# A two-layer diffusion trunk on one core: the program's blocks put in order by a timeline simulator instead of the core simulator

## The chip, the core and the metric

The kernel runs on one core of a Trainium2 chip. The metric is the device time of one execution in microseconds (us), as the median of several runs. The profile of before comes from one more execution, recorded by the hardware profiler; all starts and durations below are from it.

The engines carry their usual short names: PE is TensorE (matmuls and transposes; PEld its weight loads), DVE is VectorE, ACT is ScalarE, POOL is GpSimd, SP is SyncE, which here only issues DMAs. Each engine works through its own queue of instructions in the order in which the built program holds them; an instruction whose inputs are not ready holds up all that stand behind it in that queue.

## What is computed

One inference step of a trunk with two layers over 640 tokens: 512 sample tokens and 128 prompt tokens, model width 2048. Each layer is

```
mod   = silu(cond) @ ada_w + ada_b            # shift, scale, gate; one set for the sample, one for the prompt
h     = rms_norm(x) * (1 + scale) + shift
p     = h @ w_in                              # the columns are cut into q, k, v, gates and conv inputs
y     = concat(branches(p)) * silu(gates)
x     = x + gate * (y @ w_out)
```

The even layer (layer 0) has windowed grouped-query attention with a sink logit per head, and a gated depthwise convolution of width 3. The odd layer (layer 1) has differential attention (two softmax maps per head, an RMS norm of each head's output) and grouped-query attention with normed and rotated q and k over cached and new keys. The prompt attends to itself only. New keys and values of the prompt are outputs too.

## The kernel before

**Products.** Every float32 product is made of three float32r matmuls. `split` (L213, L214) cuts a tile into a high part, an ACT copy (L213), and a low part, a DVE subtraction (L214: `lo = x - hi`). The product is then wh times h-high, wh times h-low and wl times h-high. So each weight tile `raw` of 128x512, loaded by an SP DMA, costs one ACT copy into `wh` and one DVE subtraction into `wl` before PE can use it. The three matmuls are L248 to L250 (`proj_q`), L261 to L263 (`proj_parts`) and L526 to L528 (`run_pairs`, the output projection, which multiplies sums and differences of blocks of weights and of activations so that it needs fewer products). They accumulate in PSUM tiles `pa`, `pb`, `Sp` and `pq`, nearly always 128 by 320 (half of the tokens) to a matmul.

**Start.** The conditioning rows `rows_a` and `rows_b` are transposed on PE (L120, L121) into one PSUM tile `T`, from which DVE reads `sT`, the silu of the condition (L122), and `vec` (L123, L124). The PSUM tiles named `T` have two buffers, which every transposition of the kernel shares. `x_block` (L869 to L884) transposes x, four 128x128 blocks to a `T` (L875); L876 copies each `T` into `xT`, three of four on DVE and the fourth on ACT; L880 squares x on ACT for the norm. Then `ada_on_pe` multiplies the first ada weights (L163 loads `ada`, 1 MB a time; L166 multiplies; L169, L172 and L174 bring the result into columns). `h0_maker` (L913 to L922) makes the 16 tiles `h`; behind the last of them in the source, L922 negates the sink logits (`nsink<-sink`), which DMA brings.

**Lead stage and fill.** The input projections of layer 0 begin while the other ada blocks come in, in eight units. The remaining modulation is spread over layer 0 by `ada_on_dve` (L186 loads `adaw`, 512 KB a time into three buffers; L189 and L191 multiply and add on DVE, 240 of them L191).

**Attention.** `pair_gen` gives the steps of two heads: scores (L738 to L742), softmax (L705 and L709 on DVE, L712 on ACT, L716 and L718 on DVE, L797 on ACT), transposes of p (L726), the split of p into `pth` (ACT) and `ptl` (DVE), the weighing of v (L786 to L788). `diff_gen` (L1453 to L1475) combines the two maps of differential attention, norms the result `on` (L1460 to L1464) and transposes it back (L1470). Keys are made by a projection, transposes (L555), norm and rotation (L580 to L600) and transposes again (L608, L555), then split into `k0h`, `k0l`, `k1h`, `k1l`. In the source these steps are interleaved by hand with the projections of the next heads.

**Between the layers.** `make_form` (L1073 to L1075) makes the sums and differences for the output projection and splits them into tiles `T0` to `T7`; L1112 adds the gated result to x (`xr`); `h1_maker` (L1300, ACT L1302, L1304) makes the 16 tiles `h` of layer 1, each for several ranges of columns, from `w8`, `T1`, `T2`, `acc`, `T0` and `xr` tiles.

**What sets the order.** The source is written as generators that are stepped in turn, which fixes each instruction's place in the program. The context (`tile.TileContext`, L1647) takes each block of that program and orders it anew, engine by engine, by running it through a simulator with a model of what each instruction costs: what is ready first in the simulator, and earlier in the program, goes first. It also hands out buffers and semaphores. On the chip the order is then fixed.

## Time and profile before

| | us |
|---|---|
| median of 3 runs (2296.95 to 2298.61) | 2298.29 |
| the profiled execution | 2296.36 |
| its span, first to last instruction | 2294.5 |
| PE busy | 2255.1 |
| PE weight loads busy | 2178.4 |
| DVE busy | 1590.6 |
| ACT busy | 1089.8 |
| POOL busy | 160.5 |

The profiled execution lies 1.9 us under the median and 1.9 us over its own span. A busy time is the union of an engine's instructions in the span; matmuls overlap, so a busy PE need not be one at its best rate. The stages follow each other so: start and lead stage to about 187 us, even attention and convolution to about 930, output projection of layer 0 and the norm to about 1180, odd projections and attention to about 2085, the last output projection to the end.

### The profile page before, as it was taken

The page shows a single profiled execution, that of the slowest core. Times are in us where ns is not written, and L with a number is a line of the kernel's source. Part 1 is how long each engine was busy: PE and PEld are TensorE (multiplying, and loading weights), DVE is VectorE, ACT ScalarE, POOL GpSimd, SP SyncE. Part 2 cuts the span into 40 slices and gives each one's busy share as a digit, 9 for nine tenths or more (in the row PEclk, how much of TensorE's full clock was granted, in tenths as well). Part 3 has the DMA queues.
Part 4 walks back from the last instruction along what each step waited for, and adds up shares of the span by engine and source line. Part 5 has one row for each costly group of instructions (what it writes and reads, how often), then busy time and mean ns, then how long its engine had stood idle before and what let it go on. Part 6 is the DMA issues. An engine that isn't in the chain of part 4 may idle for free.

```text
span 2294.5 us, 41094 instructions
## 1 busy us (share of the span) xinstructions
PE 2255.1 (98%) x15900; PEld 2178.4 (95%) x15900; DVE 1590.6 (69%) x2831; ACT 1089.8 (47%) x2304; POOL 160.5 (7%) x224
## 2 busy tenths in 40 slices
PE   7999999999999999999999999999999999999999
PEld 5889899999999999999999999999999999999999
DVE  4666968779779777787796665365665655557875
ACT  5325652443522222444564443465565676755443
POOL 1001000000000000000100001011111100000101
PEclk9999999999999999999999999999999999999999
DMA  9985537547366564855553335223223211238642
GB/s 322 294 268 161 157 113 215 152 135 215 113 212 215 179 190 142 268 170 147 169 159 103 115 115 151 80 62 104 78 64 102 71 54 51 73 103 270 188 138 62
DMA packets 380900, 342.89 MB, mean 149 GB/s; under 512 B 16403, under 2 KB 338417, under 8 KB 380193
## 3 DMA queue, kind: packets, MB, share of 16 engines
q1 hardware_dynamic: 366288, 296.00, 42.9%
q0 software_dynamic: 13696, 42.10, 5.4%
q8 instruction: 125, 2.05, 0.4%
q10 hardware_dynamic: 720, 2.16, 0.3%
q14 instruction: 71, 0.57, 0.1%
HBM read 301.27 MB, written 38.93 MB: 148 GB/s over the span
## 4 chain that ended last, share of the span: by engine, by line
PE 84%; DVE 5%; ACT 4%; issue 3%; DMA 3%; POOL 1%; SPq 0%; POOLq 0%; ACTq 0%; DVEq 0%
PE pq L528 7%; PE pq L527 7%; PE pq L526 7%; PE pa L248 6%; PE pb L248 6%; PE pa L249 6%; PE pb L249 6%; PE pa L250 6%; PE pb L250 6%; PE pb L262 2%; PE pb L261 2%; PE pa L261 2%; PE pb L263 2%; PE pa L263 2%; PE pa L262 2%
## 5 line engine op out<-in xcount | busy, mean ns | idle before, releaser
L213 ACT ACTIVATE wh<-raw 128x512 fp32r<-128x512 f32 (+1 forms) x456 | 273.3, 600 | 578.4 <-PE pb L249 409.5
L214 DVE TENSOR_TENSOR wl<-raw,wh 128x512 fp32r<-128x512 f32 (+1 forms) x456 | 296.7, 652 | 214.7 <-ACT wh L213 194.2
L248 PE MATMUL pa<-h,wh 128*128 128x320 f32 x1024 | 326.0, 319 | 3.7 <-ACT h L213 2.3
L249 PE MATMUL pa<-h,wh 128*128 128x320 f32 x1024 | 319.2, 313 | 1.1 <-DVE h L214 1.0
L250 PE MATMUL pa<-h,wl 128*128 128x320 f32 x1024 | 318.7, 311 | 0.4 <-DVE wl L214 0.4
L249 PE MATMUL pb<-h,wh 128*128 128x320 f32 x1024 | 317.8, 310 | 0.0
L248 PE MATMUL pb<-h,wh 128*128 128x320 f32 x1024 | 317.6, 310 | 0.0
L250 PE MATMUL pb<-h,wl 128*128 128x320 f32 x1024 | 317.5, 310 | 0.0
L191 DVE SCALAR_TENSOR_TENSOR acc<-adaw,sT,acc 128x1024 f32<-128x1024 f32 x240 | 300.3, 1280 | 0.7 <-DMA adaw<-in_ada_w 0.7
L248 PEld LDWEIGHTS pa<-h,wh 128*128 128x128 f32 x1024 | 193.1, 189 | 17.8 <-issue 10.4
L526 PE MATMUL pq<-h,wh 128*128 128x320 f32 x640 | 199.0, 311 | 0.3 <-ACT wh L213 0.3
L249 PEld LDWEIGHTS pa<-h,wh 128*128 128x128 f32 x1024 | 193.3, 189 | 6.2 <-issue 3.3
L528 PE MATMUL pq<-h,wl 128*128 128x320 f32 x640 | 198.3, 310 | 0.1
L527 PE MATMUL pq<-h,wh 128*128 128x320 f32 x640 | 198.0, 309 | 0.0
L250 PEld LDWEIGHTS pa<-h,wl 128*128 128x128 f32 x1024 | 193.2, 189 | 2.7 <-issue 2.1
L249 PEld LDWEIGHTS pb<-h,wh 128*128 128x128 f32 x1024 | 192.6, 188 | 0.8 <-issue 0.8
L248 PEld LDWEIGHTS pb<-h,wh 128*128 128x128 f32 x1024 | 192.5, 188 | 0.7 <-issue 0.4
L250 PEld LDWEIGHTS pb<-h,wl 128*128 128x128 f32 x1024 | 192.6, 188 | 0.0
L527 PE MATMUL pq<-T,wh 128*128 128x320 f32 x480 | 148.1, 308 | 0.0
L528 PE MATMUL pq<-T,wl 128*128 128x320 f32 x480 | 147.9, 308 | 0.2 <-DVE wl L214 0.2
L526 PE MATMUL pq<-T,wh 128*128 128x320 f32 x480 | 147.8, 308 | 0.1
L261 PE MATMUL pa<-h,wh 128*128 128x320 f32 x432 | 141.2, 327 | 0.0
(431 smaller groups left out, 5311.3 us busy)
## 6 DMA issues: line engine op xcount, KB each, us to landing
adaw<-in_ada_w SPq DMA_DIRECT2D x128, 512.0 KB, 4.4
raw<-in_ev_w_in SPq DMA_DIRECT2D x176, 256.0 KB, 3.4
raw<-in_od_w_in SPq DMA_DIRECT2D x160, 256.0 KB, 2.9
ada<-in_ada_w SPq DMA_DIRECT2D x32, 1024.0 KB, 7.8
w<-in_od_w_in SPq DMA_DIRECT2D x24, 512.0 KB, 4.0
yd<-y POOLq DMA_DIRECT2D x32, 320.0 KB, 3.1
yin<-yd SPq DMA_DIRECT2D x32, 320.0 KB, 4.2
w<-yd SPq DMA_DIRECT2D x32, 320.0 KB, 4.0
```

The costliest lines, as they stand in the source:

```text
L191: V.scalar_tensor_tensor(out=acc[c], in0=w, scalar=sT[:, kt, c:c + 1], in1=acc[c], op0=ALU.mult, op1=ALU.add)
L213: A.activation(hi, x, AF.Copy)
L214: V.tensor_sub(lo, x, hi)
L248: PE.matmul(ps, wh[:, i, :], hi[:, sl], start=(j == js[0] if alone else (pos == 0 and j == 0)), stop=False)
L249: PE.matmul(ps, wh[:, i, :], lo[:, sl], start=False, stop=False)
L250: PE.matmul(ps, wl[:, i, :], hi[:, sl], start=False, stop=(j == js[1] - 1 if alone else (pos == 3 and j == 3)))
L261: PE.matmul(ps, wh[:, j, :], hi[:, sl], start=(qd == 0 and j == 0), stop=False)
L262: PE.matmul(ps, wh[:, j, :], lo[:, sl], start=False, stop=False)
L263: PE.matmul(ps, wl[:, j, :], hi[:, sl], start=False, stop=(qd == 3 and j == 3))
L526: PE.matmul(ps, wh[:, j, :], hi, start=(new and h == 0 and j == 0), stop=False, **kw)
L527: PE.matmul(ps, wh[:, j, :], lo, start=False, stop=False, **kw)
L528: PE.matmul(ps, wl[:, j, :], hi, start=False, stop=(h == 1 and j == 3), **kw)
```

## The change

One argument of the context is added. Nothing in the program's source, its tiles, pools or instructions differs.

```
-    with tile.TileContext(nc) as tc:
+    with tile.TileContext(nc, schedule_with_timeline_sim=True) as tc:
         trunk_kernel(tc, I, O)
```

The context now orders the blocks by a simulator of a timeline, with another model of costs. Both programs have the same instructions: 15533 on PE (matmuls), 2831 on DVE, 2098 on ACT, 851 DMA issues on SP, 227 on POOL. Of these, 8999 on PE stand at another place of their queue (by up to 351 places), 2157 on DVE (up to 206), 1424 on ACT (up to 60) and 571 on SP (up to 77). The moves fill the start and lead stage (the first 1000 or so PE instructions), even attention, the forms and the norm between the layers (on DVE), and odd attention; elsewhere the queues agree. Three places follow. A name's number tells one buffer's generation from another.

**DVE at the start.** Before, the three reads of `T_130` (the transposed conditioning rows) open the queue, ahead of the copies of x:

```order
L122 TENSOR_SCALAR sT_81<-T_130 128x16x2
L123 COPY vec_83<-T_130 128x80
L124 COPY vec_83<-T_130 128x77
L876 COPY xT0_206<-T_212 128x4x128
L882 TENSOR_REDUCE ssx_240<-s4_211 128x1
L883 TENSOR_SCALAR ssx_240<-ssx_240 128x1
L876 COPY xT1_207<-T_220 128x4x128
```

Now they stand behind a weight split, and behind DVE's first ten copies of x; the negation of the sink logits, whose data SP loads, comes a few rows later, ahead of the last five copies of x:

```order
L876 COPY xT0_206<-T_311 128x4x128
L214 TENSOR_TENSOR wl_459<-raw_450,wh_458 128x256
L122 TENSOR_SCALAR sT_81<-T_130 128x16x2
L123 COPY vec_83<-T_130 128x80
L124 COPY vec_83<-T_130 128x77
L214 TENSOR_TENSOR wl_463<-raw_452,wh_462 128x256
L214 TENSOR_TENSOR wl_467<-raw_454,wh_466 128x256
L922 TENSOR_SCALAR nsink_150<-sink_149 128x8
L876 COPY xT1_207<-T_319 128x4x128
L214 TENSOR_TENSOR wl_471<-raw_456,wh_470 128x256
L876 COPY xT2_208<-T_325 128x4x128
L876 COPY xT0_206<-T_344 128x4x128
```

So `sT` and the last parts of `xT`, which L166 needs, now come after `wl_459`, whose `raw_450` is a weight load, and after `sink`. `nsink` stood far behind, in the lead stage, before.

**DVE in the first pair of even attention.** Here `ptl_3102` and `ptl_3111` are splits of transposed p, which PE waits for; L191 is the modulation fill; `wl` rows split weights of later projections. Before, the rows around `ptl_3152`, the next split, are

```order
L214 TENSOR_TENSOR ptl_3152<-T_3148,pth_3151 128x256
L214 TENSOR_TENSOR wl_3392<-raw_3064,wh_3391 128x512
L971 TENSOR_TENSOR y_2595<-T_3135,y_2595 128x2x128
L716 TENSOR_TENSOR l_3127<-l_3127,es_3129 128x1
L191 SCALAR_TENSOR_TENSOR acc1_3036<-adaw_3644,sT_81,acc1_3036 128x1024
L718 RECIPROCAL rl_3132<-l_3127 128x1
L705 TENSOR_REDUCE nm_3167<-S_3159 128x1
L191 SCALAR_TENSOR_TENSOR acc0_3035<-adaw_3718,sT_81,acc0_3035 128x1024
L709 TENSOR_SCALAR nm_3167<-nm_3167,rq0_2687,nsink_150 128x1
L191 SCALAR_TENSOR_TENSOR acc1_3036<-adaw_3718,sT_81,acc1_3036 128x1024
L214 TENSOR_TENSOR ptl_3185<-T_3179,pth_3184 128x512
```

and now the rows ahead of `ptl_3102` are

```order
L191 SCALAR_TENSOR_TENSOR acc0_3035<-adaw_4098,sT_81,acc0_3035 128x1024
L214 TENSOR_TENSOR wl_3679<-raw_3545,wh_3678 128x512
L705 TENSOR_REDUCE nm_3084<-S_3075 128x1
L191 SCALAR_TENSOR_TENSOR acc1_3036<-adaw_4098,sT_81,acc1_3036 128x1024
L718 RECIPROCAL rl_3018<-l_3013 128x1
L191 SCALAR_TENSOR_TENSOR acc0_3035<-adaw_4162,sT_81,acc0_3035 128x1024
L709 TENSOR_SCALAR nm_3084<-nm_3084,rq0_2687,nsink_150 128x1
L191 SCALAR_TENSOR_TENSOR acc1_3036<-adaw_4162,sT_81,acc1_3036 128x1024
L191 SCALAR_TENSOR_TENSOR acc0_3035<-adaw_4243,sT_81,acc0_3035 128x1024
L191 SCALAR_TENSOR_TENSOR acc1_3036<-adaw_4243,sT_81,acc1_3036 128x1024
L716 TENSOR_TENSOR l_3088<-l_3088,es_3090 128x1
L214 TENSOR_TENSOR ptl_3102<-T_3096,pth_3101 128x512
```

All of L191 that stands here was further behind. Counted from the queue's start, 17 more L191, six more 128x512 L214 and three more rotations of 128x512 (L627, L629, L630) now stand ahead of `ptl_3102`, and 18, 6 and 3 ahead of `ptl_3152`. On PE, 126 more matmuls of 128x320 and 10 more of scores stand ahead of the first use of `ptl_3102`, and 114 more ahead of that of `ptl_3152`.

**PE at the keys of one head in odd attention.** `T_18649` is the last transpose of a new key (L555); `on_18687` is a normed output of differential attention; `T_18784` is the rotated key, from `m1_18658`; `S_19043` are the first scores with it. Before, 58 rows (54 of them projections) lie between `T_18649` and the transpose of `on_18687`, and 127 (117 of them projections) between `T_18784` and `S_19043`; the first of these stretches ends so:

```order
L261 MATMUL pa_18598<-h13_13311,wh_18632 128x320
L262 MATMUL pa_18598<-h13_13311,wh_18632 128x320
L263 MATMUL pa_18598<-h13_13311,wl_18633 128x320
L1470 MATMUL T_18747<-ident_78,on_18687 128x128 x2
L261 MATMUL pa_18598<-h14_13318,wh_18632 128x320
L262 MATMUL pa_18598<-h14_13318,wh_18632 128x320
```

Now 22 rows, 18 of them projections, lie between the first two, and one row between the others:

```order
L263 MATMUL pb_19018<-h15_13325,wl_19064 128x320
L1470 MATMUL T_18679<-ident_78,on_18574 128x128 x2
L1453 MATMUL T_18683<-vh_17893,pth_18623 128x256
L1454 MATMUL T_18683<-vl_17894,pth_18623 128x256
L1455 MATMUL T_18683<-vh_17893,ptl_18624 128x256
L1470 MATMUL T_18747<-ident_78,on_18687 128x128 x2
L608 MATMUL T_18779<-ident_78,ctxk_18593 128x128 x2
L555 MATMUL T_18784<-ident_78,m1_18658 128x128 x4
L555 MATMUL T_18791<-ident_78,kg_18637 128x128
L738 MATMUL S_19043<-k0h_18777,q0ah_18053 128x384
```

What stood between has moved ahead: the projections (L261 to L263) of later heads come earlier in PE's queue. Of the last 200 rows of the odd attention stage, 114 were projections before; now 5 are, and the last 191 rows hold none, only scores, transposes of p and weighings.

## The prediction

> **What bounds the kernel now.** First the page's busy times and its chain of waits:
>
> ```profile
> PE 2255.1 (98%) x15900; PEld 2178.4 (95%) x15900; DVE 1590.6 (69%) x2831; ACT 1089.8 (47%) x2304; POOL 160.5 (7%) x224
> ...
> PE 84%; DVE 5%; ACT 4%; issue 3%; DMA 3%; POOL 1%; SPq 0%; POOLq 0%; ACTq 0%; DVEq 0%
> ...
> L191 DVE SCALAR_TENSOR_TENSOR acc<-adaw,sT,acc 128x1024 f32<-128x1024 f32 x240 | 300.3, 1280 | 0.7 <-DMA adaw<-in_ada_w 0.7
> ```
>
> PE is busy 98% of the span, its weight loads 95%, and PE holds 84% of the chain. The new program has the same PE instructions, so PE's own work stays, and the question is only how long PE stands still in the new order. For that, the waits of PE, in two stretches (what waited, for whom, us in total, times, longest); of the second stretch, from 195 us to the end, the first and the last of 16 rows:
>
> ```profile
> PE T L120 <- DMA rows_a<-in_ada_b: 8.0, 1, 8.0
> PE T L121 <- DMA rows_b<-in_d_q_norm: 4.0, 1, 4.0
> ...
> PE T L555 <- DVE m L600: 4.8, 4, 1.6
> ...
> PE T L726 <- ACT p L797: 0.2, 1, 0.2
> ```
>
> The 16 rows make 17.8 us, the longest single wait 1.6 us. So no order can gain more than some 18 us behind the start; it can lose far more, since each place where PE now finds its operand just in time is one that a wrong neighbour can open. The windows tell how much room the helpers have there (stretch, its length, then busy time of PE, PEld, DVE, ACT and POOL, granted clock, DMA share, GB/s):
>
> ```profile
> 0.00:60.00 60.00, 44.21 (x368) 32.41 (x368) 27.25 (x72) 30.15 (x65) 7.15 (x17) 1.00 0.98 323
> 235.00:300.00 65.00, 63.31 (x459) 58.60 (x458) 62.27 (x116) 44.91 (x99) 4.75 (x4) 1.00 0.51 152
> 1480.00:1780.00 300.00, 296.21 (x2072) 285.15 (x2072) 185.07 (x386) 174.59 (x452) 43.01 (x54) 1.00 0.27 81
> 1780.00:2085.00 305.00, 301.27 (x2138) 292.48 (x2137) 170.27 (x326) 199.14 (x429) 25.17 (x31) 1.00 0.26 81
> ```
>
> In the first 60 us DMA is full. From 235 to 300 us DVE is as full as PE: 62.3 of 65 us. In odd attention DVE and ACT are some 60% busy; there it is not their load that can hold PE up, but the length of a chain with too little PE work beside it.
>
> The sum below is made against the profiled execution's 2296.36 us; the median is 1.93 us more, and the forecast is given for the median.
>
> **1. Start.** Single instructions (start, duration, engine, line; in brackets the idle time before and what ended it):
>
> ```profile
> 12.82 0.19 DVE L122 TENSOR_SCALAR sT<-T 128x32 f32<-128x32 f32 x1 [7.17 <-PE T L121]
> 27.09 0.69 DVE L876 COPY xT<-T 128x512 f32<-128x512 f32 x1 [0.15 <-PE T L875]
> 27.84 1.93 PE L166 MATMUL T<-ada,sT 128*32 128x256 f32 x32 [0.19 <-DVE xT L876]
> 30.57 0.78 ACT L213 ACTIVATE wh<-raw 128x256 fp32r<-128x256 f32 x2 [0.36 <-DMA raw<-in_ev_w_in]
> 31.23 0.76 DVE L214 TENSOR_TENSOR wl<-raw,wh 128x256 fp32r<-128x256 f32 x2
> 36.44 0.41 PE L248 MATMUL pa<-h,wh 128*128 128x320 f32 x1
> ```
>
> Before, `sT` was made at 12.82, the last copy of x began at 27.09 and L166 at 27.84. In the new DVE queue the three reads of `T_130` and five copies of x stand behind a split of `raw_450`. If that weight lands as before (it released ACT at 30.57), the split runs from 31.23; then the three reads (0.5), two splits (0.76), `nsink` (taken as 0.2) and five copies at 0.72 follow: 31.23 + 0.38 + 0.5 + 0.76 + 0.2 + 3.6 = 36.7, so L166 begins near 36.9, 9 us late; the DMA for `sink`, now ahead of those copies too, can only add. PE's queue then has two L166 groups ahead of the first projection, whose weights need buffers that the first groups free. What can come back: DMA goes on loading while PE stands, as far as buffers reach. I take **+10**, between 7 (part regained) and 14 (loads wait for released buffers, and DMA, 0.98 full, never catches up).
>
> **2. First pair of even attention.** DVE and PE around the two splits of p:
>
> ```profile
> 248.09 1.28 DVE L191 SCALAR_TENSOR_TENSOR acc<-adaw,sT,acc 128x1024 f32<-128x1024 f32 x1
> 249.29 0.15 DVE L716 TENSOR_TENSOR l<-l,es 128x1 f32<-128x1 f32 x1
> ...
> 253.54 1.28 DVE L214 TENSOR_TENSOR ptl<-T,pth 128x512 fp32r<-128x512 f32 x2
> ...
> 258.30 0.42 DVE L214 TENSOR_TENSOR ptl<-T,pth 128x256 fp32r<-128x256 f32 x1
> ...
> 254.85 0.28 PE L787 MATMUL T<-ptl,vh 128*128 128x256 f32 x1
> ...
> 259.48 0.28 PE L787 MATMUL T<-ptl,vh 128*128 128x256 f32 x1
> ```
>
> One L191 keeps DVE 1.20 us (248.09 to 249.29), a 128x512 L214 some 0.64 (two in 1.28). `ptl_3102` and `ptl_3111` are the two at 253.54, `ptl_3152` the one at 258.30, ready at 258.72 and used at 259.48: 0.76 us to spare. Ahead of `ptl_3152` there are now 18 more L191 and nine more 128x512 instructions: 18 x 1.20 + 9 x 0.64 = 27.4 us of DVE work. PE has 114 more projections ahead of its use; one takes 0.147 us (rows in part 4), so 16.8 us. PE waits 27.4 - 16.8 - 0.76 = 9.8 us. At `ptl_3102` the same sum gives 17 x 1.20 + 5.8 - 18.5 - 1.4 (ten scores) - 0.6 = 5.7, part of the same wait. DVE had some 2 us of 65 idle, so it can't make this up. The last steps of the pair hang on DVE too; I take **+11**, between 9 and 15 (if the fill's loads fall behind as well).
>
> **3. Forms before the layer-0 output projection.** Ahead of the seventh form (`sx_11013`) the new DVE queue has seven more L214 of 128x320, eight more L1112 and two more L1227:
>
> ```profile
> L1227 DVE TENSOR_TENSOR acc<-acc,sq 128x640 f32<-128x640 f32 x3 | 2.5, 822 | 0.0
> ...
> L1112 DVE SCALAR_TENSOR_TENSOR xr<-pb,hgt,xr 128x192 f32<-128x192 f32 (+1 forms) x6 | 2.1, 381 | 0.0
> ...
> L214 DVE TENSOR_TENSOR h<-tables,h 128x320 fp32r<-128x320 f32 x4 | 1.8, 484 | 0.0
> ```
>
> That is 7 x 0.48 + 8 x 0.38 + 2 x 0.82 = 8.0 us more, in a stretch where DVE also has idle time. Between nothing and 8, I take **+5** here, and **+4** for the same pattern ahead of the last output projection.
>
> **4. The norm of layer 1.** Rows of DVE, then of PE:
>
> ```profile
> 1146.34 0.69 DVE L214 TENSOR_TENSOR wl<-raw,wh 128x512 fp32r<-128x512 f32 x1 [0.46 <-ACT wh L213]
> ...
> 1147.83 0.35 DVE L1304 SCALAR_TENSOR_TENSOR h<-T,mod,h 128x128 fp32r<-128x128 f32 x1
> 1148.09 0.35 DVE L1300 SCALAR_TENSOR_TENSOR T<-T,gsc,sf 128x128 f32<-128x128 f32 x1
> ...
> 1149.01 0.75 DVE L1300 SCALAR_TENSOR_TENSOR T<-T,gsc,sf 128x512 f32<-128x512 f32 x1
> 1149.67 0.35 DVE L1304 SCALAR_TENSOR_TENSOR h<-T,mod,h 128x128 fp32r<-128x128 f32 x1
> ...
> 1149.88 0.31 PE L249 MATMUL pa<-h,wh 128*128 128x320 f32 x1
> 1150.02 0.31 PE L250 MATMUL pa<-h,wl 128*128 128x320 f32 x1
> ```
>
> The split at 1146.34 (`wl_13057`) is used at 1150.02. Now 14 more L1300 and L1304 of 128x512 and 15 more of 128x128 stand ahead of it, 0.66 and 0.26 us each from start to start: 13.1 us. Without the 0.46 us of idle time it ends at 1145.88 + 13.1 + 0.69 = 1159.7. PE has 21 more matmuls ahead of its use, 3.1 us (0.147 each, 1149.88 to 1150.02), so it comes at 1153.1 and waits 6.6 us. The splits behind it in the queue follow at their own pace, while PE wants one every few matmuls. I take **+10**, between 6.6 and 13.
>
> **5. Odd attention.** The chain at a new key, and that of one step of weighing:
>
> ```profile
> 1640.70 0.75 PE L555 MATMUL T<-ident,stg 128*128 128x128 f32 x5
> ...
> 1648.66 0.48 DVE L1464 SCALAR_TENSOR_TENSOR on<-on,rn,con 128x256 f32<-128x256 f32 x1
> ...
> 1650.06 0.38 PE L1470 MATMUL T<-ident,on 128*128 128x128 f32 x2
> ...
> 2064.11 0.60 PE L726 MATMUL T<-ident,p 128*128 128x128 f32 x4
> ...
> 2064.74 0.60 ACT L213 ACTIVATE pth<-T 128x512 fp32r<-128x512 f32 x1
> ...
> 2065.37 0.69 DVE L214 TENSOR_TENSOR ptl<-T,pth 128x512 fp32r<-128x512 f32 x1 [1.10 <-ACT pth L213]
> ```
>
> From the end of the key's transposes (1641.45) to the end of L1464 (1649.14) the helpers take 7.7 us, and 54 projections, 7.9 us, ran on PE meanwhile. Now 18 do, 2.6 us, and a few small matmuls, some 0.7: PE waits 4.4 at L1470. Then the rotated key is transposed and used two rows on, so its copy and its split (0.60 and 0.69) and the rows beside them lie open: some 2 more. Two heads have this pattern: +13. In a step of weighing, from the end of L726 (2064.71) to the end of `ptl` (2066.06) 1.35 us pass. In the last 191 rows no projection covers it: the weighing follows right on the transposes in one half of each step (1.35 open), and on six scores (0.12 us each) in the other (0.6 open), so about 2 us in each of some six steps: +13. For the steps between, with thinner cover than before, the bound from below is nothing and from above the tail's 2 us in each of the 20 or so; I take a third, +14. Together **+40**, between 20 and 55.
>
> **Sum.** 10 + 11 + 5 + 4 + 10 + 40 = 80; from this go 8 of the 17.8 us of old waits, which stand at neighbours that are now others. 2296.4 + 72 + 1.9 = **2370**.
>
> **PE's clock.** A window of the start shows what a standstill did to it:
>
> ```profile
> 6.00:12.00 6.00, 0.42 (x1) 0.18 (x1) 0.00 (x0) 2.67 (x6) 0.00 (x0) 1.00 1.00 348
> ```
>
> PE was busy 0.42 of these 6 us, and the granted clock stayed at 1.00; so the sum takes PE at its full rate behind each new wait. [...]
>
> **Rivals.**
>
> A, **faster**: the new order moves projections ahead, so the old waits go and no new ones come. It decides at `ptl_3152`: DVE's 27.4 us of added work would have to be under PE's 16.8. Gain at most the 17.8 us, time 2298.3 - 18 = 2280. Chance 0.05.
>
> B, **milder**: DVE and ACT, 60% busy in odd attention, run ahead and the chains there stay covered; only start, first pair and norm count, at their low ends: 10 + 10 + 7 - 6 = 21, time 2319. For it: the chain's 7.7 us holds rows of other work. Against: one row between key and scores. Chance 0.15.
>
> C, **nothing**: the moves cancel or hit idle time everywhere. Against it stand 8999 moved PE instructions. 2298; chance 0.03.
>
> D, **clock**: PE's clock falls to half in the five longest new standstills (start, pair, norm, two keys) and stays there for some time. If that time is as long as the wait at L121 above, 4.0 us, each costs 2.0 more: 10 more, 2380. Chance 0.1, since the granted clock did not fall in the window above.
>
> E, **worse**: the upper bounds of 1 to 5 hold, 14 + 15 + 16 + 13 + 55 = 113, time 2411. Chance 0.12.
>
> The forecast, with its own range 2340 to 2395, has the other 0.55. From 2318 to 2405, A, C, the lower part of B and half of E are left out, some 0.2. Faster by over 0.2% (about what a measurement of this kernel can tell from no change) is A, 0.05; within it C, 0.03; slower 0.92.
>
> **What would show it.** In the new profile: L166 begins near 37 us (1); the waits of PE name `ptl` around 260 us with 9 us or more (2), `sx` or `T` near 950 (3), `wl` or `h` near 1155 with 7 or more (4), `on` L1464 with two waits over 4 us, and `ptl` with many of about 1 us in the last 30 us of odd attention (5). PE's busy time stays within a few us. The forecast fails if the waits of PE in odd attention are under 15 us, or if a stall at one place lets DVE catch up so that the next does not come.

## The result, and the profile after

The change makes the kernel slower: 2397.57 us in the median of four runs (2396.23 to 2408.86) against 2297.62 for before (four runs), a ratio of 1.0442 with a 95% interval of 1.0424 to 1.046. That is some 100 us, where 72 were forecast (2370, range 2318 to 2405).

The page of the changed kernel, the lines that answer to those of before:

```profile
span 2394.8 us, 41182 instructions
PE 2287.0 (95%) x15900; PEld 2201.8 (92%) x15900; DVE 1592.6 (67%) x2831; ACT 1089.3 (45%) x2304; POOL 159.8 (7%) x224
...
PE 80%; issue 10%; DVE 4%; ACT 3%; DMA 2%; POOL 1%; ACTq 0%; SPq 0%; POOLq 0%; DVEq 0%
```

DVE and ACT are busy as long as before, to within 2 us. PE's share fell from 98% to 95%, but its busy time grew by 31.9 us, from 2255.1 to 2287.0, for the same instructions: the 100 us are time in which PE stands still (some 68) or runs slowly (some 32), not more work. What PE waited for, from 205 us to the end (the largest rows, and the last of 31):

```profile
PE pq L526 <- ACT wh L213: 14.4, 4, 7.0
PE T L1470 <- DVE on L1464: 8.0, 2, 4.1
PE T L786 <- DVE ptl L214: 7.6, 7, 1.3
PE S L738 <- ACT p L712: 5.9, 8, 1.5
PE T L726 <- ACT p L797: 5.4, 3, 4.4
PE T L787 <- DVE ptl L214: 5.2, 9, 2.5
...
PE T L555 <- DVE y L1475: 0.2, 1, 0.2
```

The 31 rows make 79.3 us where before's 16 made 17.8; with the start, PE's waits grew from 34.3 to 102.0 us, by 68. The windows (stretch, length, busy PE, PEld, DVE, ACT, POOL, granted clock, DMA share, GB/s) show a second thing that before hardly had, a granted clock under 1:

```profile
240.00:300.00 60.00, 51.25 (x348) 48.23 (x346) 57.96 (x83) 27.73 (x55) 1.32 (x1) 0.96 0.70 210
...
1140.00:1200.00 60.00, 49.74 (x300) 48.21 (x299) 42.33 (x94) 36.42 (x79) 6.43 (x9) 0.86 0.44 137
...
1680.00:1740.00 60.00, 54.71 (x371) 51.99 (x370) 31.91 (x71) 29.08 (x84) 8.79 (x12) 0.94 0.22 69
...
2100.00:2160.00 60.00, 49.55 (x335) 45.05 (x334) 31.71 (x62) 38.74 (x78) 3.54 (x5) 1.00 0.19 61
```

Over the span the mean clock is

```profile
core 0: 2394.8 us, clock 0.987
```

so, as the trace's record of the clock behind the start holds 1.00 and 0.50 alone, some 62 us at half rate (2 x 0.013 x 2394.8), against some 9 before (0.998). PE stood still in about 11 of the 62. In the rest projections stand 0.267 us apart in place of 0.147: by an estimate from these numbers, some 20 us more than before.

Where the time went: the two traces hold the same 15900 matmuls and transposes, and at places where PE's two queues agree, the n-th of one is the n-th of the other. How much later it starts in the changed kernel gives the loss of each stage:

| stage, its end in before | forecast | measured |
|---|---|---|
| start and lead stage, 201 us | +10 | +14.4 |
| even attention, 682 us | +11 | +11.1 |
| forms of layer 0, 1009 us | +5 | +4.9 |
| norm of layer 1, 1218 us | +10 | +12.5 |
| odd attention, 2093 us | +40 | +48.2 |
| last forms, 2175 us | +4 | +7.2 |
| old waits that go | -8 | none of its own |

In all other stretches PE runs alike in the two kernels to within 0.3 us. The six make 98.3 us; of the 100.3 us by which the span grew, 0.4 come ahead of PE's first instruction and 1.5 behind its last.

### The profile page after: what moved, and what is told of

Same layout as the page of the kernel before. It is cut to its first block, busy times and chain, and to the rows that moved or that the text cites. A ratio compares the mean times of both kernels' runs of the same rounds, so it can differ in the third digit from the quotient of the medians.

```text
span 2394.8 us, 41182 instructions
## 1 busy us (share of the span) xinstructions
PE 2287.0 (95%) x15900; PEld 2201.8 (92%) x15900; DVE 1592.6 (67%) x2831; ACT 1089.3 (45%) x2304; POOL 159.8 (7%) x224
## 4 chain that ended last, share of the span: by engine, by line
PE 80%; issue 10%; DVE 4%; ACT 3%; DMA 2%; POOL 1%; ACTq 0%; SPq 0%; POOLq 0%; DVEq 0%
PE pa L248 6%; PE pa L249 6%; PE pa L250 6%; PE pb L249 6%; PE pb L248 6%; PE pb L250 6%; PE pq L528 5%; PE pq L527 5%; PE pq L526 5%; PE pa L261 3%; PE pa L262 3%; PE pa L263 3%; PE pb L262 3%; PE pb L261 3%; PE pb L263 3%
## 5 line engine op out<-in xcount | busy, mean ns | idle before, releaser
L214 DVE TENSOR_TENSOR wl<-raw,wh 128x512 fp32r<-128x512 f32 (+1 forms) x456 | 295.8, 650 | 187.3 <-ACT wh L213 175.7
L248 PE MATMUL pa<-h,wh 128*128 128x320 f32 x1024 | 323.7, 317 | 5.1 <-ACT h L1302 3.0
L249 PE MATMUL pa<-h,wh 128*128 128x320 f32 x1024 | 319.0, 312 | 1.4 <-DVE h L1304 1.1
L191 DVE SCALAR_TENSOR_TENSOR acc<-adaw,sT,acc 128x1024 f32<-128x1024 f32 x240 | 300.1, 1275 | 1.0 <-DMA adaw<-in_ada_w 1.0
L526 PE MATMUL pq<-h,wh 128*128 128x320 f32 x640 | 200.3, 313 | 14.4 <-ACT wh L213 14.4
L705 DVE TENSOR_REDUCE nm<-S 128x1 f32<-128x768 f32 (+3 forms) x120 | 92.0, 767 | 79.9 <-PE S L740 62.6
```

The costliest lines, as they stand in the source:

```text
L191: V.scalar_tensor_tensor(out=acc[c], in0=w, scalar=sT[:, kt, c:c + 1], in1=acc[c], op0=ALU.mult, op1=ALU.add)
L214: V.tensor_sub(lo, x, hi)
L248: PE.matmul(ps, wh[:, i, :], hi[:, sl], start=(j == js[0] if alone else (pos == 0 and j == 0)), stop=False)
L249: PE.matmul(ps, wh[:, i, :], lo[:, sl], start=False, stop=False)
L526: PE.matmul(ps, wh[:, j, :], hi, start=(new and h == 0 and j == 0), stop=False, **kw)
```

## The experiments

Two theories stood against each other for most stages. **Queue theory**: PE waits because a row that it needs stands further back in a helper's queue, or, in attention, because the projections that covered a chain have moved away. **Rival**: the loss comes from another queue, the DMAs or the buffers. A third, for the size, was the clock. `hold` below adds an edge that orders two instructions of one queue and makes nobody wait; the kernel's own simulator then orders all that isn't held around these edges, so other rows shift with them:

```
+def hold(tc, order):
+    made = {i.name: i for i in tc.nc.cur_bb.bb.instructions}
+    edge = mybir.DependencyInfo(mybir.DependencyClass.NoSync, mybir.DependencyReason.DATA)
+    for first, then in order:
+        tc.add_manual_dep(made[f"I-{then}"], f"I-{first}", edge, reason="hold")
```

In "+2.6" and the like below, a stage's loss is against before, as in the table above. A single trace of before's order differs from another by up to 3 us in a stage, so smaller differences say nothing. Ten runs stand behind the time of `all_held` and five behind that of `odd_head`; the others are single runs.

**Is it the order alone?** The kernel after, with four queues in before's order:

```
+PE_ROWS, DVE_ROWS, ACT_ROWS, SP_ROWS = ...   # the numbers of before's queues
...
     with tile.TileContext(nc, schedule_with_timeline_sim=True) as tc:
         trunk_kernel(tc, I, O)
+        for rows in (PE_ROWS, DVE_ROWS, ACT_ROWS, SP_ROWS):
+            hold(tc, list(zip(rows, rows[1:])))
```

> The kernel after the change, with PE's, DVE's, ACT's and SP's queues held in the order of before, row for row. Order theory (the order of the queues is all that the change does to the time): within 3 us of before, 2295 to 2301. Rival (buffers and semaphores, which the context hands out anew, cost part of the 100 us): 2305 or more.

Measured: 2298.94 against 2297.20, ratio 1.0006 (0.9996 to 1.0016). The order of the queues is the whole of the change, with what follows from it: once the order is held, nothing else that the context hands out costs anything that shows. (Whether the buffers then came out as before isn't known.)

**The norm, one part alone.** The kernel before, DVE's rows around the norm in the new order, PE's queue as before:

```
+        hold(tc, list(zip(PE_ROWS, PE_ROWS[1:])))       # before's
+        hold(tc, list(zip(DVE_ROWS, DVE_ROWS[1:])))     # 150 rows, the change's
```

> The kernel before, with 150 DVE rows around the norm of layer 1 in the order of the change (L1300 and L1304 ahead of the weight splits); PE's order is that of before. Queue theory: PE waits 6.6 to 13 us at 1150 to 1165 us for h and wl, and loses nothing elsewhere: 2304 to 2310. Clock theory: the granted clock falls at about 1155 us and the loss is 2 to 4 us over the waits. Rival (ACT's and the DMAs' order matter, DVE's alone doesn't): under 3 us.

Measured: 2307.59 against 2298.30, the stage +12.5 as in the change. PE's timeline there (start, duration, line; the bracket is the idle time before), and windows over it:

```profile
1159.69 0.64 PE L250 MATMUL pa<-h,wl 128*128 128x320 f32 x1 [6.68 <-DVE wl L214]
1160.13 0.47 PE L248 MATMUL pa<-h,wh 128*128 128x320 f32 x1
1160.39 0.47 PE L249 MATMUL pb<-h,wh 128*128 128x320 f32 x1
1160.66 0.47 PE L250 MATMUL pb<-h,wl 128*128 128x320 f32 x1
```

```profile
1150.00:1155.00 5.00, 3.02 (x21) 2.75 (x19) 5.00 (x12) 5.00 (x13) 0.00 (x0) 1.00 0.00 0
1155.00:1160.00 5.00, 0.31 (x1) 0.31 (x2) 5.00 (x12) 5.00 (x12) 0.67 (x1) 0.50 0.00 0
1160.00:1165.00 5.00, 5.00 (x20) 5.00 (x20) 4.68 (x11) 5.00 (x12) 1.39 (x3) 0.50 0.96 259
1165.00:1170.00 5.00, 5.00 (x35) 5.00 (x34) 3.50 (x8) 3.68 (x8) 0.70 (x1) 0.98 0.78 213
```

The wait at `wl_13057` is 6.68 us; the prediction had worked out 6.6 from row counts and durations, and the split's end at 1159.7 (it ended at 1159.64). And the clock had fallen to 0.50 during the wait and stayed there until 1165: projections stand 0.265 us apart in place of 0.147, and 20 of them start in five us where 35 do at full rate.

**The clock by itself.** In the lead stage of layer 1, 240 us in which before's granted clock is 1.00 throughout and PE waits for 0.4 us in all, one ACT copy is done more often, at five places:

```
+    mark, pair_runs, STALL = [None], [], {30: 10, 52: 13, 74: 17, 96: 22, 118: 30}
...
-        split(wh, wl, raw)
+        [A.activation(wh, raw, AF.Copy) for _ in range(times)]; split(wh, wl, raw)
```

> The kernel before, with the ACT copy that makes wh done 10, 13, 17, 22 and 30 times more, once each, at five splits some 39 us apart in the lead stage of layer 1 (1190 to 1400 us), where before no clock fell. ACT works 0.63 us for each more, and PE has some 5 us of splits in hand: waits of about 1, 3, 6, 9 and 14 us. Clock theory: behind the waits of 6 us and more the granted clock falls to half, and PE loses 1 to 4 us more than the wait itself, projections standing 0.29 us apart; behind 1 us nothing. Rival (the clock has nothing to do with PE's waits): no fall there, and the loss is the wait.

Measured: 2336.21, the stage +37.9. The waits that PE has there, and windows of 20 us around them:

```profile
PE pq L526 <- ACT wh L213: 26.2, 4, 11.0
PE pq L526 <- ACT tables L507: 1.6, 1, 1.6
PE pa L250 <- DVE wl L214: 1.0, 1, 1.0
```

```profile
1200.00:1260.00 60.00, 59.04 (x403) 58.77 (x402) 41.96 (x66) 26.50 (x51) 2.69 (x5) 1.00 0.37 111
1270.00:1290.00 20.00, 17.14 (x97) 16.65 (x96) 8.40 (x13) 12.09 (x22) 1.08 (x2) 0.83 0.24 80
1315.00:1335.00 20.00, 14.76 (x89) 14.02 (x88) 9.81 (x16) 13.39 (x25) 0.54 (x1) 0.91 0.20 57
1365.00:1385.00 20.00, 11.29 (x61) 10.81 (x60) 6.85 (x9) 12.50 (x23) 0.00 (x0) 0.74 0.10 29
1415.00:1435.00 20.00, 8.98 (x49) 8.50 (x48) 4.45 (x8) 14.03 (x24) 0.75 (x2) 0.74 0.13 43
```

Ten more copies made PE wait for nothing, and a wait of 1.0 us for `wl`, at 1214 us, left the clock at 1.00 (first window). The four others made PE wait 2.9, 1.6 + 3.6, 8.7 and 11.0 us, and each time the clock fell to half: by the trace's record of the clock for 6.8, 3.4, 10.2 and 10.2 us, which the windows show as means of 0.83, 0.91, 0.74 and 0.74. The waits make 28.8 us, the loss is 37.9: by this difference, some 9 us are the clock's. The clock theory held in this run, and a fall came already with a wait of 2.9 us, where the expectation had 6.

**Odd attention, PE's queue.** Once the change with PE's rows there in before's order, once before with PE's rows there in the change's:

```
+        hold(tc, list(zip(PE_ROWS, PE_ROWS[1:])))       # 4116 rows; odd_pe: before's, odd_pe_b: the change's
```

> The kernel after the change, with PE's 4116 rows of odd attention in the order of before; the timeline simulator orders the other queues around that. Cover theory: the 46 us lost in odd attention fall to under 6 and the clock stays at 1.00 there; the other places lose as in the change: 2345 to 2360. Rival (DVE's and ACT's order by the timeline simulator loses them, whatever PE's order): 20 us or more stay there, 2370 or more.

> The kernel before, with PE's 4116 rows of odd attention in the order of the change; the other queues are ordered by the core simulator as before, around that. Cover theory (projections moved ahead leave the attention chains open): 35 to 55 us more, 2332 to 2352, with waits for on L1464 and for ptl and none before 1480 us. Rival (the loss there comes from DVE's and ACT's order under the timeline simulator; the core simulator orders them well for any order of PE): under 15 us, 2297 to 2312.

With before's order the stage loses 10.0 in place of 48.2 (2364.07 in all), and the clock does not fall there. Two windows over the stage:

```profile
1480.00:1780.00 300.00, 291.84 (x2037) 280.27 (x2035) 167.16 (x345) 164.83 (x416) 35.89 (x44) 1.00 0.25 75
1780.00:2085.00 305.00, 299.17 (x2100) 287.64 (x2099) 172.90 (x339) 196.96 (x446) 30.40 (x38) 1.00 0.25 76
```

The 10 that stay miss the 6 of the expectation, and the whole its range. With the change's order in the kernel before, the stage loses 67.9 (2368.31), more than in the change itself and more than expected. So PE's order is enough for the loss, and without it 38 of the 48 us go; and the order that the timeline simulator gives the other queues is the better one for that PE order, by 20 us.

**The fill in even attention**, again both ways: before with the fill ahead (PE's queue as before), and the change with the fill where it was (PE's queue as in the change).

```
+        hold(tc, AHEAD)      # fill_early: each of the first 70 L189/L191 ahead of the DVE row that it precedes in the change
...
+        hold(tc, BEHIND)     # fill_back: each of the 256 behind the DVE row that it follows before
```

> The kernel before, with the modulation fill (L189, L191) ahead of the DVE rows that it is ahead of in the change, for the first 70 fill rows; PE's order is that of before. Queue theory: at 250 to 300 us PE waits 9 to 15 us for ptl and for the softmax, 2306 to 2313. Rival (the fill's place costs little, the change's loss there comes from PE's and SP's new orders): under 3 us, 2295 to 2301. Clock theory: behind waits over some 4 us the granted clock falls, and the loss exceeds the waits by 1 to 4 us.

> The kernel after the change, with each of the 256 fill rows on DVE (L189, L191) behind the row that it follows before; PE's rows of even attention stay in the order of the change. Queue theory with the fill as cause: the 11.5 us lost from 200 to 500 us fall to under 4, 2385 to 2391. Rival (the weight splits and rotations that moved ahead too, with PE's new order, lose them): 7 us or more stay, 2392 or more.

The fill alone loses 22.7 us in even attention (2318.48), twice what the change loses there and more than expected. But with the fill put back the change still loses 11.7 there, and 11.2 more behind it, where PE waits 8.8 us at once for the end of the fill, which now comes too late (2411.08). PE's waits from 205 to 520 us with the fill put back:

```profile
PE S L738 <- ACT p L712: 7.3, 4, 2.7
PE T L726 <- ACT p L797: 2.5, 2, 1.7
PE T L786 <- ACT pth L213: 0.5, 1, 0.5
```

These are the softmax's steps, and ptl is gone. So the early fill is enough for the loss, but not needed: what is left of the change there, PE's new order of even attention with the splits and rotations that moved ahead on DVE, is enough too. The rival of that expectation is right; which of its two parts loses it, no run shows.

**The start**, three ways: before with DVE's new places alone (PE's queue as before); the change with the reads of `T_130` and `nsink` moved back on DVE; the change with more of the start as before.

```
+        hold(tc, [(wl_459, L122), (nsink, copy of T_319)])      # start_late, on before
...
+        hold(tc, [(L124, wl_459), (its row before, nsink)])     # start_fix, on after
...
+        hold(tc, PE: L121 first; DVE: 60 rows; ACT: 50 rows; nsink)    # start_all, on after
```

> The kernel before, with two edges on DVE's queue alone: the reads of T_130 (L122 to L124) behind the split wl_459, and nsink (L922) ahead of the last copies of x, as the change has them; PE keeps its order of before. Queue theory (PE waits because DVE's queue holds other rows ahead of what it needs): the first L166 begins near 37 us in place of 27.8, and 7 to 15 us are still missing at 200 us: 2304 to 2312. Rival (the start is set by DMA, which is full there, and PE's late start is made up by 200 us): within 3 us of before, 2295 to 2301.

> The kernel after the change, with two edges on DVE: the split wl_459 behind the reads of T_130, and nsink behind the row that it follows before. Queue theory: L166 begins near 29 us again, and the 14.9 us that the change loses by 200 us fall to 0 to 6: 2383 to 2391. Rival (PE's new order of transposes, or DMA's new order, costs them): 10 us or more of them stay, 2393 or more.

> The kernel after the change, with the start of three queues as before: on PE only L121 ahead of the transposes of x, on DVE the first 60 rows, on ACT the first 50, and nsink where it was; PE's two groups of L166 ahead of the first projection, and SP's order, stay as in the change. Slot theory (T_130 keeps one of two PSUM buffers while PE transposes x, and ACT squares x ahead of its copies): L166 begins within 2 us of 27.8 and at most 5 of the 14.9 us at 200 us stay. Rival (the order of DMAs and PE's L166 groups cost it): L166 is early again, yet 8 us or more are missing at 200 us.

Loss of the stage: 20.4 (2314.84), 18.7 (2407.25) and 11.6 (2401.12), where the change has 14.4. DVE's new places alone lose more than the whole change: L166 begins at 47.05 us, where 37 was expected. Moved back within the change they gain nothing. The reads still come behind ten copies of x, and in the change's PE order L121, the second transpose into `T_130`, is done only at 32.97 us, where before had it at 12.42; so `T_130` still keeps one of two PSUM buffers. With the start of three queues as before L166 begins early again, but then PE waits for the ada loads (waits to 205 us, then two L166 groups), and from 39.7 us the clock falls for 6.8 us (projections stand 0.27 us apart at 45 us):

```profile
PE T L166 <- DMA ada<-in_ada_w: 5.1, 4, 2.4
```

```profile
29.00 1.93 PE L166 MATMUL T<-ada,sT 128*32 128x256 f32 x32 [0.18 <-DVE xT L876]
...
41.15 1.93 PE L166 MATMUL T<-ada,sT 128*32 128x256 f32 x16 [2.39 <-DMA ada<-in_ada_w]
```

So of that expectation the slot theory is right for the late L166, and the rival for what is missing at 200 us. In the new order PE also does L166 in 31 pieces in place of 24.

**Two other orders.** PE's whole queue in the order of the source, and before with only the first 600 of PE's rows of odd attention from the change, where the change had gained 3.2 us:

```
-        trunk_kernel(tc, I, O)
+        with tc.manual_schedule(engines={mybir.EngineType.PE}):
+            trunk_kernel(tc, I, O)
...
+        hold(tc, list(zip(PE_ROWS, PE_ROWS[1:])))       # odd_head: 600 rows of the change's, then before's
```

> The kernel before with PE's whole queue in the order of the source, interleaved by hand; the core simulator orders the other queues around it. If what counts is only that attention steps have projections between them, as the source has, 2290 to 2330. If PE's order must know when operands come (theory: the loss of the change is an order made for other times), many steps stand a little too early, and it takes 2350 to 2600.

> The kernel before, with the first 600 of PE's rows of odd attention in the order of the change, where the change gained 3.2 us on before (from 1480 to 1530 us), and the rest in the order of before. If that gain is the order's own: 2293 to 2296, a ratio of 0.9985. Rival (it is bought by projections that are missing later): 2297 or more.

The source's order takes 2396.18, as long as the change and inside the second range of its expectation: some 40 us are lost in even attention and some 40 by the end of the odd one. The spliced order takes 2316.17, ratio 1.0083 (1.0069 to 1.0097). It has the 3 us of gain, and at the seam it loses them six times over. The waits there, from 1540 to 1620 us, and a window:

```profile
PE T L1470 <- DVE on L1464: 4.6, 1, 4.6
PE T L555 <- DVE m L600: 4.1, 1, 4.1
PE T L1470 <- DVE kg L582: 2.3, 1, 2.3
PE T L608 <- DVE kg L582: 1.8, 1, 1.8
```

```profile
1570.00:1610.00 40.00, 25.37 (x142) 22.05 (x141) 18.43 (x44) 18.16 (x57) 7.14 (x10) 0.70 0.27 87
```

While these waits followed each other within a few us the clock was down: a mean of 0.70 over 40 us is 24 us at half rate. Of all the orders tried none beats before.

## Why the prediction was right, and where it was too small

The direction and the six places were right, and all sizes but the start's lie within the bounds given for them; the sum was 28 us too small. The time lies just above the forecast's own range (2340 to 2395) and inside the wider one. By its steps:

- **Bound.** Half right: PE's instructions stayed, and its waits grew by 68 us. But the sign that "PE's busy time stays within a few us" failed: it grew by 31.9 us, of which falls of the clock make some 20 and the transposes of x at the start 7.6. That the waits alone come near the 72 forecast is luck; the places below don't match one by one.
- **Start.** Size +14.4 for 10, just over its upper bound of 14. L166 was forecast for 36.9; in the changed kernel's PE timeline it stands at

```profile
40.35 1.93 PE L166 MATMUL T<-ada,sT 128*32 128x256 f32 x32 [0.29 <-DVE xT L876]
```

  The mechanism was half right: the late reads hold a PSUM buffer, but without them the ada loads and the pieces of L166 lose nearly as much. The sum took the reads to wait for `raw_450` alone; in the changed kernel PE does L121, which the reads need, only at 32.56 us. And it didn't have the rate of PE: only some 5 of the 14.4 us are waits, and 7.6 are longer busy time of the 80 transposes of x (first before, then the changed kernel):

```profile
L875 PE MATMUL T<-ident,xb 128*128 128x128 f32 x80 | 13.3, 311 | 1.8 <-DVE xT L876 1.5 <-DVE ssx L882 0.2
L875 PE MATMUL T<-ident,xb 128*128 128x128 f32 x80 | 20.9, 423 | 10.4 <-DVE xT L876 6.1 <-ACT xT L876 2.6 <-DVE ssx L883 0.8
```

  In both traces these transposes stand 0.21 us apart until the trace's record of the clock begins, and 0.11 behind that. It begins at 15.8 us in before, after 14 of them, and at 39.3 us in the changed kernel, after 76. There the first 52 come in bursts of four, with waits of 0.7 to 1.2 us between them; whether that kept the rate down, no run shows.
- **Even pair.** Size right (11.1 for 11), in part by luck. The wait of 9.8 us at `ptl` did not come; the changed kernel's waits from 205 to 520 us begin with

```profile
PE T L726 <- ACT p L797: 4.9, 2, 4.4
PE T L787 <- DVE ptl L214: 2.5, 1, 2.5
```

  PE waits 7.0 us for the softmax's p and 3.6 for `ptl`. At the longest of these waits ACT had itself waited 4.2 us for DVE's `rl` (L718), which stands among the L191 too, so the fill holds PE up one step earlier than the sum had it. The clock at half rate for 6.8 us makes up some 3 us. And the fill is one cause of two: the change loses as much without it.
- **Forms.** 4.9 for 5, 7.2 for 4. The sign named `sx` or `T`; PE waited for the weights' `wh`, 7.0 us at once in layer 0. The late forms reach PE through SP: its load of that weight (L442) had waited 4.0 us for DVE's `sx` rows.
- **Norm.** 12.5 for 10. PE's waits of the changed kernel from 1140 to 1200 us:

```profile
PE pa L248 <- ACT h L1302: 3.0, 2, 2.0
PE pb L249 <- DVE h L1304: 2.2, 1, 2.2
PE T L1263 <- POOL r L1259: 1.9, 1, 1.9
PE pb L248 <- ACT h L1302: 1.7, 1, 1.7
PE pa L249 <- DVE h L1304: 1.1, 1, 1.1
PE pa L250 <- DVE wl L214: 0.2, 1, 0.2
```

  PE waits 8.0 us for `h` and hardly for `wl`, whose split stands right behind the last of them in DVE's queue; the row count gave 6.6 for that place, and DVE's order alone 6.68. Some 4 of the 12.5 us are the clock's, at half rate for 17 us in this stage in place of 3.4.
- **Odd attention.** 48.2 for 40. The two waits at `on` L1464 are 4.1 and 3.9 (forecast 4.4 each); from 2115 to 2165 us, with no projection left, the waits are 11.2 (forecast 13). All waits of the stage, to its end at 2185 us, make 41.4 where before's made 6.7. That is 35 more; the clock, at half rate for 24 us in this stage, makes some 10 of the other 13, and what the last 3 are isn't settled.
- **The deduction** of 8 for old waits was wrong: the stage losses above are net, and no stage came out shorter.
- **PE's clock.** Here a step failed: "so the sum takes PE at its full rate behind each new wait". The row that it rested on, 6 to 12 us, measured nothing: before's trace has no record of the clock ahead of 15.8 us, the window shows 1.00 where there is none, and the transposes there stood 0.21 us apart, where 0.11 was measured behind it. The changed kernel's trace shows a fall to 0.50 at each of the four waits of 3 us and more behind the start (3.9 to 7.0 us), and at several shorter ones, which cost some 20 us in all. Rival D had the fall, which no row of the prediction shows, and put it at five places of 2.0 us; the trace has a dozen. The 4.0 us that D took for the length of a fall no run shows: in the changed kernel six falls last 3.4 us, four 6.8 and one 10.2, and the twelfth goes on to the end.

Rival A (faster) fell at the place that it named: DVE's added work was not under PE's. Rival B fell because the chains in odd attention don't stay covered. Two slips in the sums change little: six steps of 2 us are 12, not 13, and rival B's low ends for the start and the pair are 7 and 9, not 10 and 10, which gives 2315. What stays open is how the start's loss divides between the half-rate transposes, the ada loads, their order on SP and L166's pieces; no run separates them.

## What to carry to other kernels

Where one engine is 98% busy, an order can only be judged by what it puts next to that engine's just-in-time operands. Count the rows ahead of an operand on the helper's queue and ahead of its use on the bound engine, before and after, multiply by durations from the trace, and compare: with DVE's order alone changed, that gave a wait of 6.6 us where 6.68 was measured. In the full change the delay often reached the bound engine under another name, so trust the size of a place more than the name of its wait. An order of queues is one whole: in the start, the even pair and odd attention, one queue in the new order with the rest from the other simulator lost more than the whole new order (20.4, 22.7 and 67.9 us against 14.4, 11.1 and 48.2), and the head of one order spliced onto the other cost 19 us. And price a new wait of PE at more than its length: in `stall_clock` 28.8 us of waits cost 37.9.

## What the runs showed of the hardware that was not expected

Short waits of PE came with a clock at half. In `stall_clock`, after 2.9 us of waiting the granted clock fell for 6.8 us, after 1.6 + 3.6 for 3.4, after 8.7 and 11.0 for 10.2 each. Part of such a stretch lay in the wait itself: in the changed kernel one of 6.8 us begins at 1005.3 us, in the wait of 7.0 us that ends at 1008.8. No sharp limit shows. Behind the first 60 us of the changed kernel, falls began within the four waits of 3 us and more (4.4, 7.0, 4.1 and 3.9 us) or less than 0.4 us behind them. Of the four waits from 2 to 3 us, those of 2.24, 2.54 and 2.65 us lay in a fall or under 2 us ahead of one, but behind that of 2.97 us, at 2225 us, the clock stayed at 1.00. A single wait of 1.0 us in `stall_clock` left the clock at 1.00; in before, falls of 3.4 us stand behind waits of 1.4 us (at 957.9 and 1135.4 us), and none behind those of 1.4, 1.6 and 1.4 us that end at 237, 408 and 1497 us. In `odd_head`, waits of 1.8 to 4.6 us close together came with 24 us at half in a window of 40 (its mean clock is 0.70).

In before and in the changed kernel PE begins at about half its later rate, and the profile's windows show 1.00 there all the same: the transposes of x stand 0.21 us apart until the trace's record of the clock begins, at 15.8 and 39.3 us, and 0.11 behind it.
